# An expert's scatter in eight pieces between the next expert's gate and up products, and the next gather ahead of the SwiGLU transposes

## The chip, the cores and the metric

One NeuronCore of a Trainium2 chip runs the whole layer in one launch. Its engines run their own instruction streams and meet at semaphores: TensorE (PE in the profile, PEld for its weight loads), VectorE (DVE), ScalarE (ACT), GpSimd (POOL), and SyncE (SP), which here only issues transfers (DMA). The metric is the device time of one execution in microseconds (us). A profile is taken of one execution; its span runs from that execution's first to its last instruction.

## The reference, cut to what matters

The layer has an attention half, which the change does not touch, and an expert half, which is computed for 512 tokens of 1024 elements in float32:

```python
def expert_choice_ffn(h, w_router, w_gate, w_up, w_down):
    B, S, D = h.shape
    cap = EC_CAPACITY_FACTOR * S // N_EXPERTS          # 64
    aff = jax.nn.softmax((h @ w_router).astype(jnp.float32), axis=-1)
    gate, idx = lax.top_k(jnp.swapaxes(aff, 1, 2), cap)
    bidx = jnp.arange(B)[:, None, None]
    xe = h[bidx, idx]
    hid = (jax.nn.silu(jnp.einsum('becd,edf->becf', xe, w_gate))
           * jnp.einsum('becd,edf->becf', xe, w_up))
    ye = jnp.einsum('becf,efd->becd', hid, w_down) * gate[..., None].astype(h.dtype)
    return jnp.zeros_like(h).at[bidx, idx].add(ye)

# in the layer:
h2 = rmsnorm(x, g_norm_ffn[l]) * (1.0 + sc2) + sh2
x = x + gt2 * expert_choice_ffn(h2, w_router[l], w_gate[l], w_up[l], w_down[l])
return rmsnorm(x, g_final)
```

There are 16 experts. Each takes its 64 best tokens, multiplies them by a gate and an up matrix of 1024 x 2048 and a down matrix of 2048 x 1024, and adds the 64 rows back into the tokens' rows.

## The kernel before

The expert half starts once the router's positions are known. Tokens lie on 128 partitions in NT = 4 tiles: `x1` is the residual, `xn` its normalised copy, `pos` the place that a token has in an expert (or none). The loop over `e` in range(16) does for each expert:

- *Selection* (L1095 to L1097, DVE): `gw`, a 0/1 matrix of tokens by 64 places, one instruction for each token tile. The tile has one buffer.
- *Gather* (L1098 to L1102, PE): `px` = selected rows of `xn`, 8 matmuls.
- *Rows* (L1103 to L1111): DVE copies px to `xe`, PE transposes it (four transposes into a `tpb` bank of PSUM), DVE scales and shifts it into `xT`, the stationary operand of gate and up. `xT` has two buffers.
- *Scatter matrix and gate values* (L1113 to L1123): PE transposes `gw`, ACT casts it to `se`; PE multiplies `gw` by the affinities, DVE copies the result to `gv`.
- *Gate and up products* (L1125 to L1135, PE): for c in 0..3 a pass over a slot of gate weights into `pg`, then a pass over a slot of up weights into `pu`, 8 matmuls each. The profile counts a float32 matmul as two.
- *SwiGLU* (L1136 to L1144): Silu on ACT, product on DVE, eight transposes on PE, copies on ACT to `hT`.
- *Down product* (L1147 to L1152, PE): four passes over four slots of down weights into `py`.
- *ye* (L1154 to L1160): DVE scales `py` by `gv` and the layer's gate into `yf`; ACT and DVE split it in two parts that a faster float32r matmul takes, `ye`.
- *Scatter* (L1161 to L1166): eight times a matmul `se` x `ye` into one of two `tpb` banks (PE), and an addition into `x1` (DVE).

Each expert's weights come in 12 transfers of 2 MB (8 for gate and up in turns, 4 for down), into a ring of nine slots of 128 x 4096 floats (`we`; L984 and L996). SP issues them in ring order, and waits with each until PE has used what lay in its slot. The ring is filled for the first time (L999) before the router is done. The last expert's down weights come in 12 smaller transfers (L990), and its down product goes by column groups (L1172 to L1205), whose scatter, final norm and output follow. The last expert has no scatter of the kind above.

The text of the loop isn't the order on the engines: the framework puts each engine's instructions in an order of its own, by a timeline that it estimates, and inserts waits where tiles are reused. So the next expert's gather already stands between the gate and up passes of the one before it.

Of the kernel before, what the change touches and what calls it, by code (L numbers as in the profile page):

```python
# [9 lines left out]
F32 = mybir.dt.float32  # L10
# [4 lines left out]
OP = mybir.AluOpType  # L15
# [86 lines left out]
def tile_block(ctx, tc, x, c, positions, w_ada, b_ada, g_norm_mix, w_in, g_q_lat, g_kv_lat, w_uq, w_ukv,  # L102
# [968 lines left out]
    with ExitStack() as pb_:  # L1071
# [4 lines left out]
        for dh in range(2):  # L1076
            SP.dma_start(gt2[64 * dh:64 * dh + 64],
                         mod_d[5 * D + 512 * dh:5 * D + 512 * dh + 512].unsqueeze(0).to_broadcast([64, 512]))
        for e in range(E_N):
# [12 lines left out]
            wd = [w_.rearrange("p (r d) -> p r d", r=4) for w_ in wl[8:]]  # L1092

            gw = wbs.tile([P, NT, 2, CAP], F32, name="gw", bufs=1)
            for j in range(NT):  # L1095
                V.tensor_scalar(gw[:, j], iota[:, None, :].to_broadcast([P, 2, CAP]), pos[:, j, e:e + 1], None,  # L1096
                                op0=OP.is_equal)  # L1097
            px = ps.tile([P, 512], F32, name="px", bufs=1)  # L1098
            for j in range(NT):
                for dh in range(2):  # L1100
                    T.matmul(px[64 * dh:64 * dh + 64], gw[:, j, 0], xn[:, j, 512 * dh:512 * dh + 512],  # L1101
                             start=j == 0, stop=j == NT - 1)  # L1102
            xe = wbs.tile([P, 4, P], F32, name="xe", bufs=1)  # L1103
            V.tensor_copy(xe, px.rearrange("q (p r) -> q r p", r=4))  # L1104
            pt = ps.tile([P, 512], F32, name="tpb", bufs=2)
            for n in range(4):
                T.transpose(pt[:, 128 * n:128 * n + 128], xe[:, n], ident)
            xT = wbs.tile([P, KD, CAP], F32, name="xT", bufs=2)
            V.tensor_tensor(xT.rearrange("p (h n) s -> p n h s", h=2), pt.rearrange("p (n h s) -> p n h s", n=4, h=2),
                            a2c.rearrange("p (h n) -> p n h", h=2)[:, :, :, None].to_broadcast([P, 4, 2, CAP]), op=OP.mult)  # L1110
            V.tensor_tensor(xT, xT, sh2c[:, :, None].to_broadcast([P, KD, CAP]), op=OP.add)  # L1111
# [12 lines left out]

            pg = ps.tile([P, 2, 512], F32, name="pg", bufs=1)  # L1125
            pu = ps.tile([P, 2, 512], F32, name="pu", bufs=1)
            for c in range(4):
                for w_, acc in ((wg[c], pg), (wu[c], pu)):
                    for r in range(2):
                        k = 2 * c + r  # L1130
                        for b in range(2):
                            for hf in range(2):
                                f0 = 1024 * b + 512 * hf
                                T.matmul(acc[64 * hf:64 * hf + 64, b], xT[:, k], w_[:, r, f0:f0 + 512],  # L1134
                                         start=k == 0, stop=k == KD - 1)  # L1135
            hid = wbs.tile([P, 2, 4, P], F32, name="hid", bufs=1)  # L1136
            hT = wbs.tile([P, 4, 4, CAP], F32, name="hT", bufs=1)
            for b in range(2):
                A.activation(hid[:, b], pg[:, b].rearrange("q (p r) -> q r p", r=4), AF.Silu)  # L1139
                V.tensor_mul(hid[:, b], hid[:, b], pu[:, b].rearrange("q (p r) -> q r p", r=4))  # L1140
                pt = ps.tile([P, 512], F32, name="tpb", bufs=2)
# [6 lines left out]
            for g in range(4):  # L1148
                for r in range(4):
                    for dh in range(2):  # L1150
                        T.matmul(py[64 * dh:64 * dh + 64], hT[:, g, r], wd[g][:, r, 512 * dh:512 * dh + 512],  # L1151
                                 start=g == 0 and r == 0, stop=g == 3 and r == 3)  # L1152

# [7 lines left out]
            for dh in range(2):  # L1161
                for j in range(NT):
                    pt = ps.tile([P, 512], F32, name="tpb", bufs=2)
# [76 lines left out]
```

## Time and profile before

| what | value |
|---|---|
| median of 3 runs (lowest, highest) | 1939.73 us (1934.15, 1940.28) |
| the profiled execution | 1937.67 us |
| its span | 1935.9 us |
| mean granted TensorE clock | 0.926 |
| busy PE, DVE, ACT, POOL | 1777.8, 739.9, 395.4, 156.0 us |
| bytes moved | 531.20 MB, mean 274 GB/s |
| expert half in the span | from 938.1 us (first gather) to the end |

The page cuts the span into 40 slices and gives the busy share of each engine in tenths, the granted clock and the bytes moved; the expert half is the last 20 slices and part of the one before. A row of a timeline gives the start, the length, engine, line, operation, `output<-input` tiles and their shapes, the number of instructions merged in it, and in brackets the idle time before it and what ended it. A row of stretches gives the start and end, the length, busy time and count for PE, PEld, DVE, ACT and POOL, then the granted clock (1.00 is full speed), the share of the 16 DMA engines' time and GB/s. A row of waits reads "engine line waited for: us in total, times, longest".

### The profile page before, as it was taken

To read this page: it belongs to the slowest core of one execution; us is meant where nothing else is said; L and a number is where in the kernel's file an instruction comes from. 1 tells how busy PE (TensorE), PEld (TensorE's weight loads), DVE (VectorE), ACT (ScalarE), POOL (GpSimd) and SP (SyncE) were. 2 spreads that over 40 slices of the span, in tenths; PEclk is the share of its full clock that TensorE was granted. 3 is DMA by queue.
4 is the path that set the end of the run, shared out by engine and by line. 5 is a ranking of instruction groups with operands and counts; after the bars stand their busy time and mean duration, and the time that the engine had idled before them with its cause. 6 is when DMAs were issued, how large, how long until landed. Compare 5 with 4: busy or idle time off the path is not lost.

```text
span 1935.9 us, 21457 instructions
## 1 busy us (share of the span) xinstructions
PE 1777.8 (92%) x8812; PEld 1058.4 (55%) x8812; DVE 739.9 (38%) x1384; ACT 395.4 (20%) x769; POOL 156.0 (8%) x140
## 2 busy tenths in 40 slices
PE   4699999999999999999699999999999999999995
PEld 1466667888888888888233333334333343333332
DVE  6567865556454354445322022211222012220213
ACT  2345643322232322333000000000000000000002
POOL 6710000020020020010200000000000000000002
PEclk7799999999999999999799988899888988889888
DMA  8346666535533234234799999999999999999983
GB/s 268 92 134 212 220 200 199 154 121 154 179 102 119 66 88 122 88 109 177 312 428 427 419 407 406 399 429 403 404 403 424 407 406 406 405 429 405 406 355 93
DMA packets 133537, 531.20 MB, mean 274 GB/s; under 512 B 16952, under 2 KB 93880, under 8 KB 105792
## 3 DMA queue, kind: packets, MB, share of 16 engines
q1 hardware_dynamic: 131360, 523.02, 70.4%
q0 software_dynamic: 2080, 6.82, 0.9%
q8 instruction: 69, 1.13, 0.2%
q14 instruction: 28, 0.23, 0.0%
HBM read 520.45 MB, written 16.17 MB: 277 GB/s over the span
## 4 chain that ended last, share of the span: by engine, by line
PE 84%; DVE 8%; DMA 3%; ACT 2%; issue 2%; SPq 1%; ACTq 0%; DVEq 0%
PE pj L459 20%; PE pg L1134 13%; PE pu L1134 11%; PE py L1151 11%; PE pj L813 5%; PE pj L554 3%; PE px L1101 3%; PE tpb L1164 2%; PE sc L554 2%; DVE x L1166 2%; PE sc L884 1%; PE tpb L1120 1%; DMA raw<-in_w_ada_dram 1%; PE sc L659 1%; DMA y<-in_x_dram 1%
## 5 line engine op out<-in xcount | busy, mean ns | idle before, releaser
L459 PE MATMUL pj<-hh,ws 128*128 128x512 f32 x1248 | 406.4, 401 | 13.7 <-ACT ws L415 8.4
L459 PEld LDWEIGHTS pj<-hh,ws 128*128 128x128 f32 x1248 | 235.7, 189 | 74.4 <-ACT ws L415 8.6
L1134 PE MATMUL pg<-we,xT 128*64 128x512 f32 x1024 | 267.4, 655 | 0.0
L459 PE MATMUL pj<-hl,ws 128*128 128x512 f32 x624 | 249.7, 400 | 3.2 <-DVE hl L449 3.2
L1134 PE MATMUL pu<-we,xT 128*64 128x512 f32 x1024 | 237.3, 592 | 0.0
L1151 PE MATMUL py<-we,hT 128*64 128x512 f32 x960 | 209.3, 594 | 2.6 <-ACT hT L1144 1.1
L416 DVE TENSOR_TENSOR ws<-raw,ws 128x1024 fp32r<-128x1024 f32 (+2 forms) x114 | 141.0, 1239 | 146.7 <-ACT ws L415 146.2
L415 ACT ACTIVATE ws<-raw 128x1024 fp32r<-128x1024 f32 (+2 forms) x114 | 117.0, 1030 | 272.2 <-PE pj L459 188.6
L1134 PEld LDWEIGHTS pg<-we,xT 128*64 128x64 f32 x1024 | 86.2, 151 | 151.8 <-issue 151.5
L1134 PEld LDWEIGHTS pu<-we,xT 128*64 128x64 f32 x1024 | 83.1, 137 | 137.9 <-issue 137.6
L1151 PEld LDWEIGHTS py<-we,hT 128*64 128x64 f32 x960 | 67.6, 137 | 134.6 <-issue 128.5
L459 PEld LDWEIGHTS pj<-hl,ws 128*128 128x128 f32 x624 | 118.1, 189 | 30.5 <-DVE hl L449 3.9
L1164 PE MATMUL tpb<-ye,se 128*128 128x512 f32 x120 | 76.8, 726 | 49.5 <-DVE ye L1160 35.8
L1140 DVE TENSOR_TENSOR hid<-hid,pu 128x512 f32<-128x512 f32 x32 | 20.6, 684 | 243.5 <-PE pu L1134 243.5
L1139 ACT ACTIVATE hid<-pg 128x512 f32<-128x512 f32 x32 | 17.4, 594 | 470.1 <-PE pg L1134 470.1
L1104 DVE COPY xe<-px 128x512 f32<-128x512 f32 x16 | 11.1, 692 | 259.0 <-PE px L1101 259.0
L1155 DVE SCALAR_TENSOR_TENSOR yf<-py,gv,gt 128x512 f32<-128x512 f32 x15 | 11.3, 751 | 221.6 <-PE py L1151 221.6
L813 PE MATMUL pj<-ws,hh 128*128 128x256 f32 x512 | 94.4, 282 | 0.0
L1164 PEld LDWEIGHTS tpb<-ye,se 128*128 128x128 f32 x120 | 31.5, 275 | 100.4 <-issue 59.1
L1166 DVE TENSOR_TENSOR x<-x,tpb 128x512 f32<-128x512 f32 x120 | 78.0, 685 | 14.9 <-PE tpb L1164 13.5
L813 PEld LDWEIGHTS pj<-ws,hh 128*128 128x128 f32 x512 | 79.3, 188 | 0.0
L1101 PE MATMUL px<-xn,gw 128*64 128x512 f32 x256 | 75.8, 613 | 2.0 <-DVE gw L1096 2.0
(331 smaller groups left out, 1941.1 us busy)
## 6 DMA issues: line engine op xcount, KB each, us to landing
we<-in_w_gate_dram SPq DMA_DIRECT2D x64, 2048.0 KB, 15.6
we<-in_w_up_dram SPq DMA_DIRECT2D x64, 2048.0 KB
we<-in_w_down_dram SPq DMA_DIRECT2D x60, 2048.0 KB, 9.3
raw<-in_w_in_dram SPq DMA_DIRECT2D x38, 1024.0 KB, 5.3
raw<-in_w_ada_dram SPq DMA_DIRECT2D x22, 1024.0 KB, 6.9
x<-bkt_d SPq DMA_DIRECT2D x104, 128.0 KB, 4.1
raw<-in_w_in_dram SPq DMA_DIRECT2D x16, 512.0 KB, 5.3
stage_d<-stage POOLq DMA_DIRECT2D x26, 256.0 KB, 4.9
```

Of the source, the lines that this page charges most:

```text
L415: A.activation(dst[:, 0], src, AF.Copy)
L416: V.tensor_sub(dst[:, 1], src, dst[:, 0].bitcast(F32))
L459: T.matmul(pu, parts[k // 4][:, a, k % 4, col:col + 128], hx[b][:, k], start=k == 0 and n == 0, stop=k == KD - 1 and n == 2)
L554: T.matmul(out_, w_(a), b_(b), start=i == 0, stop=i == n_ - 1)
L659: T.matmul(pp[hh_], q_[hh_][:, a, qs], k_[hh_][:, b], start=n == 0, stop=False)
L813: T.matmul(pu[:, 256 * j:256 * j + 256], hx[b][:, k, 128 * m:128 * m + 128], parts[k // 4][:, a, k % 4], start=k == 0 and n == 0, stop=k = ...
L1101: T.matmul(px[64 * dh:64 * dh + 64], gw[:, j, 0], xn[:, j, 512 * dh:512 * dh + 512], start=j == 0, stop=j == NT - 1)
L1134: T.matmul(acc[64 * hf:64 * hf + 64, b], xT[:, k], w_[:, r, f0:f0 + 512], start=k == 0, stop=k == KD - 1)
L1140: V.tensor_mul(hid[:, b], hid[:, b], pu[:, b].rearrange("q (p r) -> q r p", r=4))
L1151: T.matmul(py[64 * dh:64 * dh + 64], hT[:, g, r], wd[g][:, r, 512 * dh:512 * dh + 512], start=g == 0 and r == 0, stop=g == 3 and r == 3)
L1164: T.matmul(pt, se[:, j], ye[:, dh], start=True, stop=True)
L1166: V.tensor_add(x1[:, j, ds_], x1[:, j, ds_], pt)
```

## The change

The selection, the gather, the rows and a piece of the scatter become functions of their own, and the loop calls them at other places: the first expert's selection, gather and rows ahead of its products; each later expert's selection and gather in the expert before it, after the SwiGLU products and ahead of their transposes, and its rows behind the first pass of the down product. The scatter of an expert moves into the next one: after each of the eight passes of gate and up stands one of its eight pieces. The scatter matrix and gate values of an expert now come after its gate and up passes. Nothing in what is computed changes; the additions into `x1` come in another order of column halves and tiles, on different elements.

```diff
+        def scatter(se, ye, j, dh):
+            pt = ps.tile([P, 512], F32, name="tpb", bufs=2)
+            T.matmul(pt, se[:, j], ye[:, dh], start=True, stop=True)
+            ds_ = slice(512 * dh, 512 * dh + 512)
+            V.tensor_add(x1[:, j, ds_], x1[:, j, ds_], pt)
+
         for e in range(E_N):
...
-            gw = wbs.tile([P, NT, 2, CAP], F32, name="gw", bufs=1)
...
-            V.tensor_tensor(xT, xT, sh2c[:, :, None].to_broadcast([P, KD, CAP]), op=OP.add)
+            if e == 0:
+                gw = select(0)
+                xT = rows(gather(0, gw))
+
+            pg = ps.tile([P, 2, 512], F32, name="pg", bufs=1)
+            pu = ps.tile([P, 2, 512], F32, name="pu", bufs=1)
+            for c in range(4):
+                for i, (w_, acc) in enumerate(((wg[c], pg), (wu[c], pu))):
+                    for r in range(2):
...
+                                T.matmul(acc[64 * hf:64 * hf + 64, b], xT[:, k], w_[:, r, f0:f0 + 512],
+                                         start=k == 0, stop=k == KD - 1)
+                    if e:
+                        scatter(se, ye, c, i)
...
             for b in range(2):
                 A.activation(hid[:, b], pg[:, b].rearrange("q (p r) -> q r p", r=4), AF.Silu)
                 V.tensor_mul(hid[:, b], hid[:, b], pu[:, b].rearrange("q (p r) -> q r p", r=4))
+            if e < E_N - 1:
+                gw = select(e + 1)
+                px = gather(e + 1, gw)
+            for b in range(2):
                 pt = ps.tile([P, 512], F32, name="tpb", bufs=2)
                 for n in range(4):
                     T.transpose(pt[:, 128 * n:128 * n + 128], hid[:, b, n], ident)
...
+                if g == 0:
+                    xT = rows(px)
...
-            for dh in range(2):
-                for j in range(NT):
-                    pt = ps.tile([P, 512], F32, name="tpb", bufs=2)
-                    T.matmul(pt, se[:, j], ye[:, dh], start=True, stop=True)
-                    ds_ = slice(512 * dh, 512 * dh + 512)
-                    V.tensor_add(x1[:, j, ds_], x1[:, j, ds_], pt)
```

`select`, `gather` and `rows` hold the lines of before word for word (L1094 to L1111). In the changed kernel the lines are: selection L1084, gather L1092, xe L1099, its transposes L1102, xT L1104 and L1106, scatter L1111 and L1113, gate and up L1142, transposes of gw L1149, gate values L1154 and L1157, SwiGLU L1161, L1162 and L1169, down L1177, yf and ye L1183 to L1188.

What the framework makes of it is seen in the engines' orders. First TensorE, where one expert ends and the next (here the fourth) begins. Before:

```order
L1151 MATMUL py<-we_7950,hT 64x512 x8
L1164 MATMUL tpb<-ye,se 128x512 x8
L1107 MATMUL tpb<-cs,xe 128x128 x4
L1115 MATMUL tpb<-cs,gw 128x128 x4
L1120 MATMUL tpb<-aff,gw 128x1 x4
L1134 MATMUL pg<-we_8138,xT 64x512 x8
L1134 MATMUL pu<-we_8140,xT 64x512 x8
```

The same place in the changed kernel (`we_` with a number is a slot's content):

```order
L1177 MATMUL py<-we_7950,hT 64x512 x8
L1142 MATMUL pg<-we_8138,xT 64x512 x8
L1111 MATMUL tpb<-ye,se 128x512 x4
L1142 MATMUL pu<-we_8140,xT 64x512 x8
L1111 MATMUL tpb<-ye,se 128x512 x4
L1142 MATMUL pg<-we_8142,xT 64x512 x8
L1149 MATMUL tpb<-cs,gw 128x128 x4
L1154 MATMUL tpb<-aff,gw 128x1 x4
L1092 MATMUL px<-xn,gw 64x512 x4
L1142 MATMUL pu<-we_8144,xT 64x512 x8
L1092 MATMUL px<-xn,gw 64x512 x4
L1142 MATMUL pg<-we_8146,xT 64x512 x8
```

The down product is followed at once by the next gate pass. The eight pieces of the scatter come in two groups of four behind the first two passes, not one behind each; the transposes of gw and the gate values stand behind the third pass, and the gather beside the fourth. In every other expert the groups are 2, 4 and 2, and the gather is one group of eight behind the fourth pass. The second expert alone has its pieces spread over passes three to eight.

Then TensorE around the down product, before:

```order
L1134 MATMUL pg<-we_8150,xT 64x512 x8
L1101 MATMUL px<-xn,gw 64x512 x3
L1134 MATMUL pu<-we_8152,xT 64x512 x8
L1101 MATMUL px<-xn,gw 64x512 x5
L1143 MATMUL tpb<-cs,hid 128x128 x8
L1151 MATMUL py<-we_8154,hT 64x512 x8
L1151 MATMUL py<-we_8156,hT 64x512 x8
```

and in the changed kernel:

```order
L1142 MATMUL pg<-we_8150,xT 64x512 x8
L1142 MATMUL pu<-we_8152,xT 64x512 x8
L1169 MATMUL tpb<-cs,hid 128x128 x8
L1177 MATMUL py<-we_8154,hT 64x512 x8
L1102 MATMUL tpb<-cs,xe 128x128 x4
L1177 MATMUL py<-we_8156,hT 64x512 x8
```

The gather has left the last passes, and the transposes of xe, which stood behind the scatter, now stand behind the first down pass. Last, VectorE over one expert, before:

```order
L1155 SCALAR_TENSOR_TENSOR yf<-py,gv,gt_7523 128x512
L1160 TENSOR_TENSOR ye<-yf,ye 64x512 x2
L1166 TENSOR_TENSOR x_67<-x_67,tpb 128x512 x8
L1109 TENSOR_TENSOR xT<-tpb,a2c 128x4x2x64
L1111 TENSOR_TENSOR xT<-xT,sh2c 128x512
L1123 COPY gv<-tpb 128x1
L1096 TENSOR_SCALAR gw<-cs,pos 128x128 x4
L1104 COPY xe<-px 128x512
```

and in the changed kernel:

```order
L1183 SCALAR_TENSOR_TENSOR yf<-py,gv,gt_7523 128x512
L1188 TENSOR_TENSOR ye<-yf,ye 64x512 x2
L1113 TENSOR_TENSOR x_67<-x_67,tpb 128x512 x8
L1157 COPY gv<-tpb 128x1
L1084 TENSOR_SCALAR gw<-cs,pos 128x128 x4
L1099 COPY xe<-px 128x512
L1162 TENSOR_TENSOR hid<-hid,pu 128x512 x2
L1104 TENSOR_TENSOR xT<-tpb,a2c 128x4x2x64
L1106 TENSOR_TENSOR xT<-xT,sh2c 128x512
```

The two steps that make xT have moved from between scatter and gate values to behind the SwiGLU product (`hid`). SP's order of transfers, and POOL's instructions, are the same in both kernels.

More of the change, by code (lines that the diff above doesn't have):

```diff
@@ L1078, in tile_block, with select, gather, rows @@
                          mod_d[5 * D + 512 * dh:5 * D + 512 * dh + 512].unsqueeze(0).to_broadcast([64, 512]))
+        def select(e):
+            gw = wbs.tile([P, NT, 2, CAP], F32, name="gw", bufs=1)
+            for j in range(NT):
+                V.tensor_scalar(gw[:, j], iota[:, None, :].to_broadcast([P, 2, CAP]), pos[:, j, e:e + 1], None,
+                                op0=OP.is_equal)
+            return gw
+        def gather(e, gw):
+            px = ps.tile([P, 512], F32, name="px", bufs=1)
+            for j in range(NT):
+                for dh in range(2):
+                    T.matmul(px[64 * dh:64 * dh + 64], gw[:, j, 0], xn[:, j, 512 * dh:512 * dh + 512],
+                             start=j == 0, stop=j == NT - 1)
+            return px
+        def rows(px):
+            xe = wbs.tile([P, 4, P], F32, name="xe", bufs=1)
+            V.tensor_copy(xe, px.rearrange("q (p r) -> q r p", r=4))
+            pt = ps.tile([P, 512], F32, name="tpb", bufs=2)
+            for n in range(4):
+                T.transpose(pt[:, 128 * n:128 * n + 128], xe[:, n], ident)
+            xT = wbs.tile([P, KD, CAP], F32, name="xT", bufs=2)
+            V.tensor_tensor(xT.rearrange("p (h n) s -> p n h s", h=2), pt.rearrange("p (n h s) -> p n h s", n=4, h=2),
+                            a2c.rearrange("p (h n) -> p n h", h=2)[:, :, :, None].to_broadcast([P, 4, 2, CAP]), op=OP.mult)
+            V.tensor_tensor(xT, xT, sh2c[:, :, None].to_broadcast([P, KD, CAP]), op=OP.add)
+            return xT
+        def scatter(se, ye, j, dh):
+            pt = ps.tile([P, 512], F32, name="tpb", bufs=2)
+            T.matmul(pt, se[:, j], ye[:, dh], start=True, stop=True)
+            ds_ = slice(512 * dh, 512 * dh + 512)
+            V.tensor_add(x1[:, j, ds_], x1[:, j, ds_], pt)
         for e in range(E_N):
@@ L1092, in tile_block @@
             wd = [w_.rearrange("p (r d) -> p r d", r=4) for w_ in wl[8:]]
[L1094 to L1111 removed]
+            if e == 0:
[6 more added lines that the diff above has]
+                    for r in range(2):
+                        k = 2 * c + r
+                        for b in range(2):
+                            for hf in range(2):
+                                f0 = 1024 * b + 512 * hf
+                                T.matmul(acc[64 * hf:64 * hf + 64, b], xT[:, k], w_[:, r, f0:f0 + 512],
+                                         start=k == 0, stop=k == KD - 1)
+                    if e:
+                        scatter(se, ye, c, i)
             pt = ps.tile([P, 512], F32, name="tpb", bufs=2)
@@ L1140, in tile_block @@
                 V.tensor_mul(hid[:, b], hid[:, b], pu[:, b].rearrange("q (p r) -> q r p", r=4))
+            if e < E_N - 1:
+                gw = select(e + 1)
+                px = gather(e + 1, gw)
+            for b in range(2):
                 pt = ps.tile([P, 512], F32, name="tpb", bufs=2)
```

14 lines of the change are left out of this document (removed).

## The prediction

> **What bounds the kernel now.** The page's slices come first, for the stage; the sequence of 16 experts fills the second half of the span. The reader should see that in it the DMA row is at 9 and the rate about 400 to 430 GB/s, while PE is at 9 as well.
>
> ```profile
> PE   4699999999999999999699999999999999999995
> DMA  8346666535533234234799999999999999999983
> GB/s 268 92 134 212 220 200 199 154 121 154 179 102 119 66 88 122 88 109 177 312 428 427 419 407 406 399 429 403 404 403 424 407 406 406 405 429 405 406 355 93
> ```
>
> Two resources look full, so the second view is the chain of waits over one expert, for its period and its pieces (start, length, what).
>
> ```profile
> 1678.46 1.80 PE tpb L1120 x8
> ...
> 1739.90 1.80 PE tpb L1120 x8
> 1741.69 5.25 PE pg L1134 x16
> 1746.94 3.43 PE pu L1134 x16
> ...
> 1771.03 3.45 PE pu L1134 x16
> 1774.57 0.70 DVE hid L1140
> 1776.69 13.98 PE py L1151 x64
> 1790.70 0.76 DVE yf L1155
> ...
> 1793.03 0.78 PE tpb L1164
> ...
> 1799.36 1.11 PE tpb L1107 x4
> 1800.48 0.85 PE tpb L1115 x4
> ```
>
> The period is 1739.90 − 1678.46 = 61.44 us, and PE's own chain carries all of it. After the end of py (1776.69 + 13.98 = 1790.67) the next pg pass starts at 1741.69 + 61.44 = 1803.13: for 12.5 us PE does no weight matmul. They are 2.36 us until ye is there, 6.33 us of scatter (1793.03 to 1799.36) and 3.8 us of transposes and gv. Then the first pg pass takes 5.25 where each later one takes 3.43.
>
> The third view, stretches of 2 us (near the end of a row: granted clock, DMA share, GB/s), tells both halves of the story.
>
> ```profile
> 1742.00:1744.00 2.00, 2.00 (x6) 0.47 (x4) 0.67 (x4) 0.00 (x0) 0.00 (x0) 0.50 1.00 426
> ...
> 1746.00:1748.00 2.00, 2.00 (x12) 0.62 (x10) 0.00 (x0) 0.00 (x0) 0.00 (x0) 1.00 0.38 107
> ...
> 1792.00:1794.00 2.00, 0.97 (x2) 0.50 (x2) 1.53 (x3) 0.80 (x2) 0.00 (x0) 0.70 0.98 418
> 1794.00:1796.00 2.00, 1.62 (x3) 0.58 (x2) 1.71 (x3) 0.00 (x0) 0.00 (x0) 0.50 1.00 426
> ```
>
> The clock falls to 0.50 in the scatter and is still there in the first pg pass. And the DMA engines run dry once per expert, here from 1746 on. Why they do is in SP's queue and in the table of waits:
>
> ```profile
> 1746.98 7.20 SPq L996 DMA_DIRECT2D we<-in_w_down_dram  x3
> SPq L996 <- PE pg L1134: 320.9, 30, 32.2
> PEld pu L1134 <- DMA we<-in_w_down_dram: 0.3, 1, 0.3
> ```
>
> SP waits for PE to free a slot of the ring of nine (320.9 us at this line alone); PE almost never waits for a transfer (0.3 us). PE frees nothing between the end of py and the end of the first pg pass, 12.5 + 5.25 us, and the queue empties. So the bound is PE's sequence, with the transfers 4% behind it. That "4%" needs their undisturbed rate: stretches without a dry spot, first and last of the twelve that lie between 1077 and 1806:
>
> ```profile
> 1077.00:1130.00 53.00, 49.52 (x206) 18.60 (x204) 11.83 (x21) 4.00 (x7) 0.00 (x0) 0.88 1.01 428
> ...
> 1751.00:1806.00 55.00, 50.59 (x214) 21.69 (x212) 11.57 (x21) 4.06 (x7) 0.00 (x0) 0.88 1.01 429
> ```
>
> A slot is 128 x 4096 x 4 bytes = 2.097 MB; at 428.5 GB/s 4.894 us, twelve of them 58.73 us per expert. The new kernel cannot go below that.
>
> **PE's period after the change.** The order listing shows the scatter as two groups of four, behind the first pg and the first pu pass (or 2, 4, 2). The prices at full clock are from the first expert, where these steps took less than in the chain above, and from the fastest scatter matmul (the first of its three durations):
>
> ```profile
> 944.89 0.66 PE L1107 MATMUL tpb<-cs,xe 128*128 128x128 f32 x4 [0.78 <-DVE xe L1104]
> 945.38 0.60 PE L1115 MATMUL tpb<-cs,gw 128*128 128x128 f32 x4
> 946.40 1.05 PE L1120 MATMUL tpb<-aff,gw 128*128 128x1 f32 x8 [0.42 <-DVE xT L1109]
> 947.57 0.87 DVE L1096 TENSOR_SCALAR gw<-cs,pos 128x128 f32<-128x128 f32 x4
> L1164 PE MATMUL tpb<-ye,se x120: 390/776/796, 996.1 to 1859.8; 128*128 128x512 f32 x120
> 975.07 3.43 PE px L1101 x16
> 1793.03 1.19 PE L1164 MATMUL tpb<-ye,se 128*128 128x512 f32 x2 [2.39 <-DVE ye L1160]
> 1793.84 1.28 DVE L1166 TENSOR_TENSOR x<-x,tpb 128x512 f32<-128x512 f32 x2 [0.23 <-PE tpb L1164]
> ```
>
> - Unchanged: 8 x 3.43 = 27.4 of gate and up, 13.98 of down, 3.43 of px, 2.2 from the last pu to py (1774.48 to 1776.69).
> - The 2.36 us until ye go to nothing: they run beside the first pg pass (3.43). Were that cover gone they would cost 15 x 2.36 = 35 us.
> - Scatter: with two tpb buffers the third piece waits for the first add. A group of four is then 0.39 + 2 x 0.64 (two adds) + 0.39, some 2.2 us with a little latency; at the pace of before, two pieces per 1.6 us, it is 3.0. Two groups are 4.4 to 6.0; I take 5.0, nearer the warm row, since weight matmuls surround them.
> - Transposes and gv: 0.66 + 0.60 + 1.05 = 2.3.
> - A new wait: gw has one buffer, so the next gather waits for gv to have read it and for the first selections (0.87 for four). In half of the experts px stands right behind gv, with pu, pg and all later PE work queued behind it: 0.2 to 1.1 us, I take 0.5. DVE's xe copy waits for px ahead of the SwiGLU product, which isn't due until the last pu.
> - The first pg pass at full clock: 5.25 becomes 3.43, −1.82.
>
> The sum is 27.4 + 13.98 + 3.43 + 2.2 + 5.0 + 2.3 + 0.5 = 54.8 us, with the ends 53.9 to 56.4. That is below 58.73, so what is late next is the transfer: PE overtakes its lead in the course of the experts and then waits for weights, some 1.5 us at a slot (4.894 − 3.43). SP's own order of issues, POOL's work and every transfer's size stay as they were; nothing is moved past either queue.
>
> **The time, then, is the transfers' path.** Its ends are read from these rows (SP's queue, stretches, PE):
>
> ```profile
> 951.08 7.19 SPq L996 DMA_DIRECT2D we<-in_w_down_dram  x3
> 950.00:955.00 5.00, 5.00 (x26) 1.72 (x24) 0.00 (x0) 0.00 (x0) 0.00 (x0) 1.00 0.59 200
> 1871.00:1874.00 3.00, 3.00 (x18) 0.98 (x16) 0.00 (x0) 0.00 (x0) 0.00 (x0) 1.00 0.89 313
> 1892.00:1895.00 3.00, 2.14 (x13) 0.68 (x10) 1.03 (x2) 0.00 (x0) 0.00 (x0) 1.00 0.86 272
> 1910.12 1.95 PE L1182 MATMUL py<-we,hT 128*64 128x256 f32 x16
> ```
>
> The first nine slots are filled before the stage. The tenth is issued at 951.08, when the first pg pass ends; the first expert is ordered as before up to there, so this stays. Data flow from 952.05 (0.59 of the five microseconds). 179 whole slots follow (192 less nine less the last four): 179 x 4.894 = 876.0, to 1828.1. The final gain's 0.52 MB adds 1.2. The last four slots, in twelve smaller transfers, took 1871.3 to 1894.6, 23.3 us: to 1852.6; about 1 us to be seen, as at the start. The last slot is first used at 1910.12, and from there to the span's end it is 1935.9 − 1910.1 = 25.8. Span 1879.4. The profiled execution took 1937.67, that is 1.8 more than its span, and 2.1 less than the median of the runs shown; so **1881 us**, 58 below that median. Per expert 2.7 us of dry queue go, some 40 in all; the other 16 or so come from the end: when the last transfer landed, PE still had all four slots of down weights before it, and now will have one.
>
> PE must also be in time: the second expert's pg starts at 994.4 instead of 1005.26, from
>
> ```profile
> 979.76 13.98 PE py L1151 x64
> ...
> 1005.26 3.58 PE pg L1134 x16
> 1896.10 7.09 PE L1182 MATMUL py<-we,hT 128*64 128x512 f32 x32
> ```
>
> and 979.76 + 13.98 + 0.66; fourteen periods p, the last expert's 36.3 up to its py (27.4 + 5.0 + 1.65 + 2.2) and 39.8 (1896.10 to the end) make 1070.5 + 14 p. PE sets the end only if p is over 57.8.
>
> **The clock, where it could go wrong.** The trace shows that PE idle for 2.39 us, followed by a scatter with gaps, costs the full clock, and that 2.2 us with transposes in it (1774.48 to 1776.69) do not. A starved PE idles 1.5 us in 4.9, less than either. In the Trainium skill, "TensorE: Matmul & The Clock Gate", section "HAM oscillation — how this bites in real kernels", bursts of matmuls that a transfer wait of over 3.4 us parts start each at half clock, which speaks against a kernel that waits for its weights. By it waits of 1.5 us cost nothing and the sum stays; were it to bite at 1.5 us too, twelve cold passes would make p 54.8 + 12 x 1.82 = 76.6. The trace is already stricter than the page, as its clock fell after 2.39 us.
>
> **Rivals.**
> 1. *Interrupted passes run cold.* Each such pass costs 1.82 us (5.25 against 3.43). With two or three per expert p is 58.4 to 60.3 and the span 1888 to 1915. For it: the first pg pass of today. Against: every gap is now framed by passes of 3.43 us at full rate. 13%, 1890 to 1917 us.
> 2. *The same, slower than before.* If both scatter groups, the gather's wait, the step to py and the ye hand-over each make a pass cold, p is 54.8 + 5 x 1.82 = 63.9 and the time 1967. It decides at p = 61.8, nearly four cold passes. But a PE that is late isn't starved, which takes starvation off the list. 5%.
> 3. *The change frees nothing.* The dry spot is not PE's doing, or the scheduler's order gives it back: 1938. SP's waits for PE and the listing speak against it. 5%.
> 4. *Deeper queues run slower.* Transfers now land 15.6 us after their issue, three slots' time, as the page has it:
>
> ```profile
> we<-in_w_gate_dram SPq DMA_DIRECT2D x64, 2048.0 KB, 15.6
> ```
>
> Up to nine will stand in line. A loss of 1 or 2% is 9 to 18 us: 1890 to 1899. 4%.
> 5. *They run faster.* A queue that never empties may gain as it may lose; 1.5% are 13 us, and with an end 3 us shorter (the groups ahead of the last slot are done by then) the time is 1865. No stretch of 50 us shows it. 4%. In the Trainium skill, "DMA: Bandwidth & Descriptors", section "Specifications", the fabric's ceiling is 435 GB/s, 1.5% above the measured 428.5, and by it 179 slots would take 13 us less.
>
> **The numbers.** My forecast has 69%, and its own range is 1872 to 1890. The likeliest time is 1881. To hold 8 in 10 the range takes in a third to a half of rival 1 and most of rival 4: 1866 to 1908. Under 0.3% (6 us) this kernel's measurement cannot tell a difference: faster 0.90, same 0.05, slower 0.05.
>
> **What would show it.** Right: DMA share 1.0 without dry spots from 952 on, its end near 1853; a period of 54 to 56 us early and 58.7 late; PE waiting for DMA of we in the later experts; clock 1.0 in nearly all stretches; SP's 320.9 us gone. Wrong: periods of 58 to 61 with the clock at 0.5 behind the scatter groups; a share of 1.0 with fewer GB/s; px waiting on gw for over 1.1 us.

## The result, and the profile after

The changed kernel takes 1887.74 us, the median of 4 runs (1883.85 to 1889.47); the kernel before took 1940.01 us beside it (4 runs, 1934.15 to 1940.9). The ratio is 0.9734, with a 95% interval of 0.9709 to 0.9759. Run again beside two of the later experiments it took 1884.85 against 1936.75 us, ratio 0.9732 (0.9715 to 0.9748). The profiled execution took 1883.85 us, with a span of 1882.1 us and a mean granted clock of 0.978 (0.926 before).

First the page's slices of the changed kernel, as they were read of before:

```profile
PE   4699999999999999999699999999988998889985
PEclk7799999999999999999799999999999999999998
DMA  9346766535534233231879999999999999999996
GB/s 273 89 130 197 244 194 191 179 107 162 166 112 126 90 90 104 90 90 68 363 331 427 426 428 428 428 426 427 428 428 427 427 428 428 428 427 427 427 424 203
```

In the second half the rate no longer swings between 399 and 429 GB/s; it stands at 424 to 428 in every full slice. PE has fallen from 9 to 8 in six slices late in the span: it is PE that waits now. The table of waits says for whom (SP's queue, then PE; us in total, times, longest):

```profile
SPq L984 <- DMA we<-in_w_down_dram: 159.8, 39, 5.8
...
SPq L996 <- PE pg L1142: 74.7, 15, 32.0
...
PE py L1177 <- DMA we<-in_w_down_dram: 18.4, 17, 2.2
PE pg L1142 <- DMA we<-in_w_gate_dram: 14.7, 12, 1.3
...
PE pu L1142 <- DMA we<-in_w_up_dram: 6.0, 8, 1.3
```

SP's 320.9 us of waiting for PE's gate passes at the down slots (L996) have become 74.7. PE waits 39.1 us for weights, in 37 waits, where it waited next to nothing. More than half of SP's other waiting is now put down to an earlier transfer: one lands 37.2 us after its issue (15.6 before), which is 37.2 / 4.89 = 7.6 transfers in line.

The chain of waits gives the periods. From the changed kernel, the starts of the first pg pass of five experts, between two of them one scatter group and the new wait for gw, and a pass that stands out:

```profile
1050.24 3.43 PE pg L1142 x16
...
1104.37 3.43 PE pg L1142 x16
1107.80 0.45 PE tpb L1111
...
1110.12 3.58 PE pu L1142 x16
...
1120.19 0.80 PE tpb L1154 x8
...
1121.17 0.20 DVE gw L1084
...
1121.42 1.94 PE px L1092 x8
...
1159.18 3.43 PE pg L1142 x16
...
1286.43 5.30 PE pu L1142 x16
...
1564.43 3.65 PE pg L1142 x16
...
1682.19 3.65 PE pg L1142 x16
```

The early periods are 54.1 and 54.8 us (1050.24, 1104.37, 1159.18); the late ones, where PE waits for weights, are (1682.19 − 1564.43) / 2 = 58.9 us, the twelve transfers of an expert. The first pg pass takes 3.43, not 5.25. One pass of the whole stage is cold, the pu pass at 1286.43; it is the only place between 955 and 1825 us where the granted clock of ten us is under 0.95. A scatter group takes 1110.12 − 1107.80 = 2.3 us. The ye that it needs was finished beside the pg pass, as the timeline has it (1105.92 + 1.40 = 1107.32):

```profile
1105.92 1.40 DVE L1188 TENSOR_TENSOR ye<-yf,ye 64x512 fp32r<-64x512 f32 x2 [0.76 <-ACT ye L1187]
```

Last, the two ends of the expert stage: SP's issue of the tenth slot, the last up slot in the chain, and PE's rows behind it.

```profile
950.32 7.19 SPq L996 DMA_DIRECT2D we<-in_w_down_dram  x3
...
1800.87 35.50 DMA we<-in_w_up_dram
...
1836.41 3.65 PE L1142 MATMUL pu<-we,xT 128*64 128x512 f32 x16 [1.26 <-DMA we<-in_w_up_dram]
1840.93 1.25 PE L1169 MATMUL tpb<-cs,hid 128*128 128x128 f32 x8 [0.86 <-DVE hid L1162]
1842.31 7.09 PE L1204 MATMUL py<-we,hT 128*64 128x512 f32 x32
1850.31 1.95 PE L1204 MATMUL py<-we,hT 128*64 128x256 f32 x16 [0.91 <-DVE yf L1206]
```

After the last up slot has landed (1800.87 + 35.50 = 1836.37), PE waits for no transfer any more: the brackets name only DVE. From there to the end of the span are 45.7 us.

From SP's issue of the tenth slot to the end are 1882.1 − 950.32 = 931.8 us; before it was 1935.9 − 951.08 = 984.8. This length is a better yardstick than the time for what follows. In the four profiles of the changed kernel and its near relatives (below) it is 931.7, 931.8, 931.8 and 931.9, while the tenth slot is issued anywhere from 948.87 to 952.44; over all profiles of this study with whole slots that point lies between 948.87 and 957.50 us. So the spread of a few us from one execution to the next seems to come from the part ahead of the experts, which is the same in all of them.

### The profile page after: what moved, and what is told of

The parts are those of the page before. It is cut to its first block, busy times and chain, and to the rows that moved or that the text cites. A ratio compares the mean times of both kernels' runs of the same rounds, so it can differ in the third digit from the quotient of the medians.

```text
span 1882.1 us, 21443 instructions
## 1 busy us (share of the span) xinstructions
PE 1716.5 (91%) x8812; PEld 996.9 (53%) x8812; DVE 738.9 (39%) x1384; ACT 395.3 (21%) x769; POOL 155.4 (8%) x140
## 4 chain that ended last, share of the span: by engine, by line
PE 64%; DMA 25%; DVE 6%; SPq 2%; issue 1%; ACT 1%; ACTq 0%; DVEq 0%; POOL 0%; POOLq 0%
PE pj L459 21%; DMA we<-in_w_up_dram 11%; DMA we<-in_w_gate_dram 10%; PE pu L1142 8%; PE pg L1142 8%; PE pj L813 5%; PE py L1177 4%; PE pj L554 3%; PE px L1092 2%; PE sc L554 2%; DVE x L1113 2%; PE sc L884 2%; PE tpb L1111 1%; DMA x<-bkt_d 1%; DMA raw<-in_w_ada_dram 1%
## 5 line engine op out<-in xcount | busy, mean ns | idle before, releaser
L1142 PE MATMUL pg<-we,xT 128*64 128x512 f32 x1024 | 233.4, 595 | 14.7 <-DMA we<-in_w_gate_dram 14.7
L1142 PE MATMUL pu<-we,xT 128*64 128x512 f32 x1024 | 236.7, 599 | 6.0 <-DMA we<-in_w_up_dram 6.0
L1177 PE MATMUL py<-we,hT 128*64 128x512 f32 x960 | 216.3, 597 | 20.3 <-DMA we<-in_w_down_dram 18.4
L1142 PEld LDWEIGHTS pg<-we,xT 128*64 128x64 f32 x1024 | 73.0, 137 | 156.2 <-issue 131.0
L1142 PEld LDWEIGHTS pu<-we,xT 128*64 128x64 f32 x1024 | 72.3, 137 | 147.8 <-issue 133.4
L1177 PEld LDWEIGHTS py<-we,hT 128*64 128x64 f32 x960 | 66.4, 137 | 150.3 <-issue 126.9
L1113 DVE TENSOR_TENSOR x<-x,tpb 128x512 f32<-128x512 f32 x120 | 77.4, 685 | 127.4 <-PE tpb L1111 127.4
L1162 DVE TENSOR_TENSOR hid<-hid,pu 128x512 f32<-128x512 f32 x32 | 20.6, 684 | 219.1 <-PE pu L1142 219.1
L1161 ACT ACTIVATE hid<-pg 128x512 f32<-128x512 f32 x32 | 17.4, 595 | 299.1 <-PE pg L1142 299.1
L1183 DVE SCALAR_TENSOR_TENSOR yf<-py,gv,gt 128x512 f32<-128x512 f32 x15 | 11.3, 751 | 155.2 <-PE py L1177 155.2
L1187 ACT ACTIVATE ye<-yf 64x512 fp32r<-64x512 f32 x30 | 18.8, 628 | 252.1 <-DVE yf L1183 251.7
L813 PE MATMUL pj<-ws,hl 128*128 128x256 f32 x256 | 71.6, 280 | 0.0
L1092 PE MATMUL px<-xn,gw 128*64 128x512 f32 x256 | 61.2, 614 | 4.6 <-DVE gw L1084 4.6
## 6 DMA issues: line engine op xcount, KB each, us to landing
we<-in_w_gate_dram SPq DMA_DIRECT2D x64, 2048.0 KB, 37.2
```

What stands on the lines that cost most here:

```text
L813: T.matmul(pu[:, 256 * j:256 * j + 256], hx[b][:, k, 128 * m:128 * m + 128], parts[k // 4][:, a, k % 4], start=k == 0 and n == 0, stop=k = ...
L1113: V.tensor_add(x1[:, j, ds_], x1[:, j, ds_], pt)
```

## Experiments: which edit frees the products

The order of the instructions on PE, read after the result was known, suggested that the place given to the scatter's pieces might not be what mattered. A `tpb` bank is handed out in the order of the text. Before, the next expert's rows (the transposes of `xe`, L1107) ask for a tpb bank *behind* the scatter's eight pieces, so they, and with them all of the next expert's products, must come after the scatter. The *turn theory* says that this turn alone made the block; the *placing theory* says that the block goes only if the scatter is written between the products. Four kernels tell them apart. (The kernel before took 1937.42 us beside these four.)

**rows_last**: the changed kernel with its early gather, but the scatter in one block and the rows called behind it.

```diff
-                    if e:
-                        scatter(se, ye, c, i)
...
-                if g == 0:
-                    xT = rows(px)
...
+            for dh in range(2):
+                for j in range(NT):
+                    scatter(se, ye, j, dh)
+            xT = rows(px)
```

> The changed kernel with its functions and its early gather, but with the scatter called in one block behind ye and the rows called behind the scatter. Theory (turn): the transposes of xe stand behind the scatter's pieces in the turns of tpb again, the engines' order is that of the kernel before, and the time is 1932 to 1945 us. Rival (placing; the early gather has a part of its own): 1890 to 1925 us.

Measured: 1939.92 us, ratio 1.0009 (0.9994 to 1.0024). The gain is gone, though selection and gather stand early. On PE stands, between the down product of one expert and the next expert's products:

```
L1175 MATMUL py<-we_7764,hT 64x512 x8
L1111 MATMUL tpb<-ye,se 128x512 x8
L1102 MATMUL tpb<-cs,xe 128x128 x4
...
L1142 MATMUL pg<-we_7952,xT 64x512 x8
```

SP waits for PE as it did before (table of waits):

```profile
SPq L996 <- PE pg L1142: 323.6, 30, 31.8
```

**gather_only**: the changed kernel with the scatter in one block behind ye, but the rows left where the change has them (the first and the third piece of the diff above, without the second and without the last line).

> Only the selection, gather and rows are moved ahead; the scatter stands in one block at the end of its own expert. Theory (turn): the rows have had their turn in tpb before the scatter starts, so the framework mixes the scatter with the next expert's passes by itself: 1882 to 1894 us. Rival (placing): the scatter in one block keeps the 12 us gap at the hand-over: 1925 to 1940 us.

Measured: 1886.08 us, ratio 0.9742 (0.9725 to 0.9759), 931.9 us from the tenth issue to the end. With the rows' turn ahead of the scatter, the framework spreads the pieces between the next expert's passes by itself; on PE stand now

```
L1175 MATMUL py<-we_7760,hT 64x512 x6
L1102 MATMUL tpb<-cs,xe 128x128 x4
L1175 MATMUL py<-we_7760,hT 64x512 x2
L1175 MATMUL py<-we_7762,hT 64x512 x8
L1175 MATMUL py<-we_7764,hT 64x512 x8
L1142 MATMUL pg<-we_7952,xT 64x512 x8
L1111 MATMUL tpb<-ye,se 128x512 x2
L1142 MATMUL pu<-we_7954,xT 64x512 x8
L1111 MATMUL tpb<-ye,se 128x512 x3
```

**scatter_only**: the changed kernel with selection, gather and rows back at the head of the loop; only the scatter's pieces stay between the next expert's passes, and with them, behind the expert's own passes, its scatter matrix and gate values.

> Only the scatter is moved into the next expert's products; selection, gather and rows stand at the head of each expert as before. Theory (turn): the rows are ahead of the scatter in the turns of tpb, which is all that counts: 1882 to 1894 us, as the changed kernel. Rival (two parts that add up): some of the gain is the gather's, 1895 to 1920 us.

Measured: 1883.68 us, ratio 0.9735 (0.972 to 0.9751), 931.7 us. Either half of the change is enough, and both together bring no more: what they share is that the rows get their bank ahead of the scatter. They share the place of the scatter matrix and gate values too, but so does rows_last, which gains nothing.

**rows_py**: the kernel before, with one line changed: the rows' transposes use py's bank, which is free once yf is made, instead of a tpb bank.

```diff
-            pt = ps.tile([P, 512], F32, name="tpb", bufs=2)
+            pt = ps.tile([P, 512], F32, name="py", bufs=1)
             for n in range(4):
                 T.transpose(pt[:, 128 * n:128 * n + 128], xe[:, n], ident)
```

> The kernel before with one word changed: the four transposes of xe take their PSUM bank from py and not from the two tpb banks. Theory (turn): what kept the scatter in one block was that those transposes stood behind the scatter's eight pieces in the turns of tpb, so that xT, and with it every product of the next expert, had to wait for the last addition; freed of that the framework itself sets the scatter between the next expert's passes. Then PE's period is 54 to 57 us, the transfers bound the expert half and the time is 1884 to 1896 us. Rival (placing): the gain comes from the scatter written between the products and the early gather, which this kernel does not have: 1936 to 1942 us.

Measured: 1899.86 us, ratio 0.9803 (0.9782 to 0.9823). The turn theory is right in its direction, but the time lies above the 1884 to 1896 us that it had been given: the gain is not quite three quarters of the whole. Why the rest is missing, this kernel's chain, PE's timeline and a stretch (granted clock third from the end) show:

```profile
1509.44 13.98 PE py L1151 x64
...
1568.11 13.98 PE py L1151 x64
...
1586.51 6.62 PE pg L1134 x16
```

```profile
1524.25 0.66 PE L1107 MATMUL py<-cs,xe 128*128 128x128 f32 x4 [0.85 <-DVE yf L1155]
1526.41 0.73 PE L1164 MATMUL tpb<-ye,se 128*128 128x512 f32 x2 [1.50 <-DVE ye L1160]
1527.85 5.24 PE L1134 MATMUL pg<-we,xT 128*64 128x512 f32 x16 [0.71 <-DVE xT L1111]
```

```profile
1528.00:1530.00 2.00, 2.00 (x6) 0.62 (x8) 0.99 (x2) 0.00 (x0) 0.00 (x0) 0.50 0.98 418
```

From the end of py (1509.44 + 13.98) to the next pg pass are now 4.4 us instead of 12.5. In them PE idles three times, 0.85, 1.50 and 0.71 us, and works for 1.4; the clock falls to 0.50, and the pass behind runs cold, 5.24 us here and 6.62 in the next expert. The period is 1568.11 − 1509.44 = 58.7 us, so PE is no faster than the transfers. This is the first rival of the prediction, in a kernel in which its condition holds, with one such pass in each expert.

The transfers lose nothing by it: from 955 to 1825 us the share of busy DMA engines is 1.00, and the last transfer lands as long after the tenth issue as in the changed kernel, 908 us. But PE never catches up with them. The last up pass starts without a wait for its slot,

```profile
1854.96 3.60 PE L1134 MATMUL pu<-we,xT 128*64 128x512 f32 x16
```

which is 1854.96 − 955.92 = 899.0 us after this kernel's tenth issue, against 886.1 in the changed kernel. So the 13 us that are missing (the stage takes 944.9 us instead of 931.8) all lie at the end.

## Experiments: how much of it is the clock

The block costs in two ways: 12.5 us in which no weights are used, and the half clock in it and behind it. Two kernels keep the block and only keep PE busy in it.

**before_warm**: the kernel before, with two fill matmuls while PE waits for ye, and each scatter matmul done a second time, into px's bank.

```diff
+            fill = ps.tile([P, 512], F32, name="px", bufs=1)
+            for _ in range(2):
+                T.matmul(fill, ident, yf, start=True, stop=True)
...
                     T.matmul(pt, se[:, j], ye[:, dh], start=True, stop=True)
+                    T.matmul(fill, se[:, j], ye[:, dh], start=True, stop=True)
```

> The kernel before with PE kept busy in the hand-over: two matmuls of yf with the identity and a second copy of each scatter matmul, written to the px bank and read by nobody. They also push the gather into the scatter's block. Theory: of the 7 us by which PE's period fell, about 3 are the clock (first pg pass 1.8, transposes and gv 1.5); with them PE's period is 57 to 60 us and the time 1886 to 1915 us. Rival (the clock has no part, only the order has): the added work keeps the period at 61 us or makes it longer, 1935 to 1970 us.

Measured: 1892.41 us beside 1940.61, ratio 0.9754 (0.9728 to 0.978). But since px's bank is taken, the next gather moved into the block too (3.61 us of px at 1518.26, between scatter and rows), which leaves PE less to do later. So the clock isn't alone in this run, and it decides nothing by itself.

**before_fill**: the same idea with the fills in pg's bank, which is free until the next pg pass; the gather stays where it was.

```diff
+            fill = ps.tile([P, 2, 512], F32, name="pg", bufs=1)
+            for b in range(2):
+                T.matmul(fill[:, b], ident, yf, start=True, stop=True)
...
                     V.tensor_add(x1[:, j, ds_], x1[:, j, ds_], pt)
+                    if (dh, j) != (1, NT - 1):
+                        T.matmul(fill[:, 0, :256], ident, x1[:, j, 512 * dh:512 * dh + 256], start=True, stop=True)
```

> The kernel before, with the scatter in one block and the gather where it was; PE only gets 2 fill matmuls of 128x512 while it waits for ye and one of 128x256 after each of the first seven additions, all into pg's bank, which the next pg pass overwrites. If the cold clock is the larger part of what the block costs: the clock stays at 1.0 from the end of py to the next pg pass, that pass takes 3.4 to 3.6 us instead of 5.25, the scatter's eight pieces take some 5 to 6 us instead of 6.33, the period is 57.5 to 59.5 instead of 61.44 and the time 1886 to 1910. If the gather's move into the block was what gained in the run with the fillers in px: the period stays over 60.5 and the time is 1925 to 1950.

Measured: 1903.11 us beside 1936.75, ratio 0.9827 (0.9808 to 0.9847). In its chain and in one of its stretches:

```profile
1515.38 13.98 PE py L1151 x64
...
1541.30 3.58 PE pg L1134 x16
...
1600.55 3.58 PE pg L1134 x16
```

```profile
1534.00:1536.00 2.00, 1.88 (x10) 1.24 (x8) 1.48 (x3) 0.00 (x0) 0.00 (x0) 1.00 1.00 426
```

The block is as long as before (1515.38 + 13.98 to 1541.30 is 11.9 us against 12.5), but the clock stays at 1.00 in it, and the pass behind it takes 3.58. The period is 59.25 us instead of 61.44, and the stage is 32.6 us shorter than before (its tenth slot was issued at 955.04: 1907.2 − 955.04 = 952.2, against 984.8). So keeping the clock up is enough for some 33 of the 53 us, with the block still there; the other 20 come only when the block itself goes, and PE runs ahead until the transfers bind. The nine fill matmuls per expert that bring these 33 us make nothing that is used.

Where the gains lie is seen from the moment at which the transfers end. These are the last stretches of 1 us in which they still move (share of busy engines before the last number), in the kernel before, rows_py, before_fill and the changed kernel:

```profile
1894.00:1895.00 1.00, 0.28 (x3) 0.29 (x4) 1.00 (x2) 0.00 (x0) 0.00 (x0) 1.00 0.38 118
1863.00:1864.00 1.00, 1.00 (x8) 0.42 (x6) 0.00 (x0) 0.00 (x0) 0.00 (x0) 1.00 0.19 61
1865.00:1866.00 1.00, 0.16 (x2) 0.00 (x0) 0.72 (x2) 0.00 (x0) 0.00 (x0) 1.00 0.80 253
1857.00:1858.00 1.00, 1.00 (x12) 0.57 (x8) 1.00 (x2) 0.94 (x3) 1.00 (x2) 1.00 0.36 119
```

| kernel | tenth issue to the end of the transfers | from there to the end |
|---|---|---|
| before | 944 us | 41 us |
| rows_py (short block, clock falls) | 908 us | 37 us |
| before_fill (long block, clock stays) | 911 us | 41 us |
| changed | 908 us | 24 us |

Either remedy alone gives the transfers back nearly all of their 36 us, so the parts of clock and block don't add up. The 17 us at the end came, of these four, only in the changed kernel, where PE is faster than the transfers and has worked off its lag when the last of them lands.

## Experiments: what bounds the changed kernel

**gather_x2** and **gather_x3**: the changed kernel with the gather of experts 1 to 15 done two and three times over into the same bank, 3.43 us of PE work more per expert each time.

```diff
-            for j in range(NT):
-                for dh in range(2):
+            for _ in range(2 if e else 1):
+                for j in range(NT):
+                    for dh in range(2):
```

> The changed kernel with the gather of experts 1 to 15 done twice (the second result replaces the first, which is the same): 3.43 us more of PE work in each of 15 experts, 51 us in all. Theory (the transfers bound it): PE's period goes from 54.4 to 57.8 us, which is the point where PE would begin to set the end; the time rises by 0 to 5 us against the changed kernel (1884 to 1893 us). Rival (PE's work bounds it): plus 45 to 55 us, about 1937 us.

> As before with the gather done three times: 6.9 us more of PE work in each expert, 103 us in all. Theory (the transfers bound it, slack of 3.4 us per expert): PE's period is 61.3 us, PE is the bound, and the span is 993.7 + 6.9 + 14 x 61.3 + 76.1 = 1935 us: about 1937 us, plus 50 against the changed kernel. Rival (PE's work bounds it already): plus 95 to 105 us, about 1990 us.

Measured, beside 1940.61 us: gather_x2 1887.35 us, ratio 0.972 (0.9703 to 0.9737), and gather_x3 1940.66 us, ratio 1.0008 (0.9993 to 1.0022). The first pg passes in their chains (gather_x2, then gather_x3):

```profile
1058.46 3.43 PE pg L1143 x16
...
1116.47 3.43 PE pg L1143 x16
...
1174.70 3.43 PE pg L1143 x16
```

```profile
1498.47 3.43 PE pg L1143 x16
...
1560.17 3.43 PE pg L1143 x16
```

At a period of 58.0 to 58.2 us nearly all of the additional work is free (the stage takes 935.7 us instead of 931.8, for 51 us of matmuls); at 61.7 us all of the gain is gone. So PE has some 4 us in hand per expert, what lies between its own 54.8 and the transfers' 58.7.

**eleven_loads**: the changed kernel with one transfer less per expert; its down product reads the third slot twice.

```diff
+                if n == 11 and e < E_N - 1:
+                    wl.append(wl[10])
+                    continue
```

> The changed kernel without the fourth down transfer of experts 0 to 14 (its passes read the third slot again, so a part of the down product is another one): 15 transfers of 2 MB less, PE's work the same. Theory (the transfers bound it, PE close behind): the transfers' path would end 74 us earlier, PE's path with its period of 54.4 us gives a span of 993.7 + 14 x 54.4 + 76.1 = 1831 us: 1828 to 1840 us. Rival a (PE is the bound): no change, 1884 to 1890 us. Rival b (nothing but the transfers counts): 1810 to 1818 us.

Measured: 1837.33 us beside 1940.61, ratio 0.9458 (0.9439 to 0.9477), 1832.0 − 950.58 = 881.4 us for the stage. Its chain has a period of 54.1 us late in the stage:

```profile
1539.92 3.43 PE pg L1145 x16
...
1594.04 3.43 PE pg L1145 x16
```

That is 50 us less for 15 transfers less, and the period is PE's own again. Both directions agree: the changed kernel is bound by its transfers, and PE follows 4 us per expert behind.

**ring19**: a try to beat it. The ring of nine slots is cut into nineteen halves, so that half a slot more is loaded ahead and the first half comes free sooner. To make room, `xe` shares the buffer of `yf`, `xT` has one buffer instead of two, and `hid` is made in two halves.

```diff
-        wb = [ctx.enter_context(pool(f"wb{n}")) for n in range(9)]
+        wb = [ctx.enter_context(pool(f"wb{n}")) for n in range(19)]
...
-            return wb[n].tile([P, 4096], F32, name=f"we{n}")
+            return wb[n].tile([P, 2048], F32, name=f"we{n}")
```

> The changed kernel with its ring of nine slots cut into nineteen halves (transfers of 1 MB): half a slot more (2.45 us of transfer) is loaded ahead, and the first half is free one half pass (1.7 us) earlier. If the transfers' path sets the whole time, the dry time ahead of the tenth slot shrinks by about 4 us, and so does the span: 1876 to 1880, the time 1878 to 1885 beside the changed kernel's 1884 to 1889, ratio to the kernel before some 0.971. If transfers of half the size cost rate (0.5% is 4.4 us), or PE still sets a part of the time: the same as the changed kernel, or up to 8 us above it.

**after_again**: the changed kernel beside it.

> The changed kernel again, as the comparison on this chip: 1883 to 1890, ratio to the kernel before 0.971 to 0.976; the transfers of the expert stage end near 1856 and start near 950.

Measured, beside 1936.75 us: ring19 1896.19 us, ratio 0.9792 (0.9768 to 0.9816); the changed kernel 1884.85 us, as above. The stretch from 955 to 1825 us of both, ring19 first:

```profile
955.00:1825.00 870.00, 802.85 (x3612) 273.03 (x3608) 174.56 (x311) 61.64 (x105) 2.43 (x4) 1.00 1.01 421
```

```profile
955.00:1825.00 870.00, 802.43 (x3640) 281.88 (x3636) 172.86 (x311) 60.73 (x105) 2.44 (x4) 1.00 1.01 428
```

The transfers did start earlier (87 GB/s from 945 to 950 us, where the changed kernel moves nothing), but transfers of 1 MB with 8 KB per partition cost 1.7% of the rate, 421 against 428 GB/s at the same share of busy time, some 14 us over the stage; size and line length changed together, so this run doesn't tell which of the two it is. The expectation had put that loss at 0.5%, and the time ended above both of its cases. Nor do the additional slots lengthen the line: a transfer of down weights lands 19.8 us after its issue, which is 19.8 / 2.49 = 8 of these transfers, and in the changed kernel the longest takes 39.4 us, 8 of 2 MB. There the ring of nine slots may be the reason, in ring19 it can't be; what holds back the ninth transfer in ring19 no run here shows. No version here that does all of the work is clearly faster than the changed kernel.

**last_whole**: a test of the one term of the prediction that was off, the end of the transfers. The last down weights come in whole slots, so the last down product takes other columns of them.

```diff
-            elif e == E_N - 1:
-                for m in range(2):
...
             else:
                 k = 512 * (n - 8)
```

> The changed kernel with the last expert's down weights in four whole transfers of 2 MB with 16 KB lines instead of twelve small ones; its down product then takes other columns of the weights. In the changed kernel the last up slot lands at 1836.4, and transfers end near 1856.5. If the twelve small transfers, which share the engines with the last whole slots, delay these: the last up slot lands 2 to 6 us earlier after the transfers' start, transfers end near 1850 to 1853 at 420 GB/s and more, and the span is 2 to 6 us shorter (1876 to 1880), the time 1878 to 1884. If the last up slot's landing is set by the ring and the sum of the whole slots alone: it lands within 1 us of 1836.4, the end is PE's work behind it, 45.7 us, and the span stays at 1881 to 1883, the time 1883 to 1888.

Measured: 1888.41 us beside 1937.77, ratio 0.9742 (0.9719 to 0.9765). The profiled execution got to the tenth slot late, at 957.50, so it is read from there. The queue's row, the last up pass, and the last stretches (share and GB/s at the end):

```profile
957.50 3.77 SPq L988 DMA_DIRECT2D we<-in_w_down_dram  x2
```

```profile
1843.63 3.65 PE L1134 MATMUL pu<-we,xT 128*64 128x512 f32 x16 [1.24 <-DMA we<-in_w_up_dram]
```

```profile
1852.00:1855.00 3.00, 2.67 (x14) 0.89 (x12) 0.00 (x0) 0.00 (x0) 0.00 (x0) 1.00 1.02 426
1855.00:1858.00 3.00, 2.17 (x11) 0.52 (x6) 0.74 (x1) 0.00 (x0) 0.00 (x0) 1.00 0.77 328
1858.00:1861.00 3.00, 2.21 (x16) 1.36 (x18) 0.70 (x2) 0.63 (x1) 0.00 (x0) 1.00 0.49 208
1861.00:1864.00 3.00, 3.00 (x22) 1.62 (x18) 0.84 (x2) 0.12 (x1) 0.01 (x1) 1.00 0.15 66
```

The last up slot is used 1843.63 − 957.50 = 886.1 us after the tenth issue, and in the changed kernel 1836.41 − 950.32 = 886.1: the small transfers don't delay it, and the first theory falls. But the second had the end wrong too: the stage is 934.4 us long, 2.6 more than with the small transfers. PE idles 1.62 us until ye is there, a time that it fills with the next column group where that comes in small pieces, and waits 0.33 us for a down slot. What the stretches show besides is how the transfers end: not at once, but over some 9 us, in which the share of busy engines falls from 1.02 to 0.15. In the changed kernel the same is seen at its last whole slot, whose packets of 16 KB can be told from those of the small transfers behind it (the DMA view of short windows counts packets under 8 KB). Small packets move from 1829 us on (of the 146 packets up to 1831, 108 are under 8 KB, and only 13 of these, of other kinds, under 512 B), and packets of 16 KB still start after 1835, 2 of the 165 up to 1836; at 1836.4 the slot has landed. So the next transfers are under way for 7 us while the last parts of the slot come in.

## Why the prediction was right, step by step

- **The bound.** Right. PE's block starved SP's queue; with the block gone the dry spots are gone, and of the wait of 320.9 us 74.7 are left, 32.0 of them a single wait.
- **PE's period.** Predicted 54.8 us, measured 54.1 to 54.8. Its terms held one by one: two scatter groups 4.6 us for 5.0, the wait on gw 0.43 us (from 1120.19 + 0.80 to 1121.42) for 0.5, the wait for ye under the first pg pass, and that pass at 3.43.
- **The transfers' period.** Predicted 58.73 us, measured 58.9 late in the stage.
- **The two parts of the gain.** Predicted were some 40 us of dry queue and 16 at the end; the transfers end 36 us earlier after the tenth issue, and what lies behind them is 17 us shorter.
- **The clock.** The forecast took waits of some 1.5 us for a slot as harmless, and they were: with 37 waits of up to 2.2 us, the clock of the whole stretch from 955 to 1825 is 1.00. The one cold pass, of 5.30 us, followed a scatter group and the transposes of gw, not a wait for weights; the same steps with the same 0.55 us of idle time were followed by a pass of 3.58 us at 1070.11. The first rival's mechanism is real, as rows_py shows, but its condition, several idle spots in a row with little between them, doesn't come up here. The two kernels also bound the Trainium skill's rule of over 3.4 us ("TensorE: Matmul & The Clock Gate", section "HAM oscillation — how this bites in real kernels"): single waits of up to 2.2 us are harmless, as it has it, but three of at most 1.50 us within 4.4 were not. The next section of that page, "A second HAM failure mode: psum-queue depth-cycling", has frequent micro-idles as a cause of its own, and rows_py with its three idle spots agrees.
- **The second rival's point of turning.** Predicted at a period of 61.8 us; gather_x3 runs at 61.7 and takes the time of before.
- **Deeper queues** run neither slower nor faster: 428 GB/s with 7.6 transfers in line, 428.5 before.
- **The sum.** The stage was to last 1879.4 − 951.08 = 928.3 us and lasted 931.8. The step that was off is "The last four slots, in twelve smaller transfers, took 1871.3 to 1894.6, 23.3 us: to 1852.6", with the 25.8 us that were added behind it. The count of bytes is right, but not the moment at which a slot has landed: by the count the last up slot is there 878 us after the tenth issue, and it was used after 886.1. The first packets of the small transfers do move at 879 us (1829 − 950.32), but alongside the last of the whole slots, as last_whole's paragraph shows, and from there to 908 us, or 1858 and not 1852.6, the last four slots took some 29 us, not 23.3. And the end hangs on that up slot, with 45.7 us of work behind it: 886.1 + 45.7 = 931.8. The last down pieces, on which the sum was built, come just in time to cost nothing; that both ways agree within 4 us is partly luck. Of the 6.7 us between 1881 and 1887.74 the other 3.9 lie between the profiled execution and the median. For the kernel before the prediction named 2.1 us between these two, but its 1881 is the span plus 1.8, the time of a profiled execution, to which they were not added.
- **What the prediction didn't see** is which words of the change do it. It costed the scatter at its new place; the experiments show that the place is the framework's choice, and that the edit counts because the rows take their tpb bank ahead of the scatter.

Open stays what exactly makes PE's clock fall: 4.4 us with 1.4 of work in them did it in rows_py, the 2.2 us of the SwiGLU step with its transposes never, and a scatter group and the transposes and narrow matmuls of gw, with 0.55 us of idle time between them, did it once and not at other times.

## What to carry to other kernels

When work of one round blocks the next round, look for the buffer or bank that both take in turn before moving any code: the turn follows the order of the text, and one line that gives the next round's first step a bank of its own, or its turn earlier, can free everything behind it. Where the freed step then meets the next limit, here the transfers 4 us further on, nothing more is to be had on that engine, as 51 us of doubled work for almost nothing showed. And a gap in front of a long run of matmuls can cost twice, as time and as clock, and the two parts need not add up: here filling the gap with matmuls that nobody uses gave 33 of the 53 us, and closing most of it while the clock still fell gave 40.

## What the runs showed of the hardware

- The granted clock reacted to what PE did in the gap, not to its length alone: 11.9 us filled with small matmuls kept 1.00 (before_fill), 4.4 us with three idle spots of at most 1.50 gave 0.50 (rows_py).
- Transfers of 2 MB with 16 KB per partition moved 428 GB/s, those of 1 MB with 8 KB 421; with the last expert's small transfers, of 1 or 2 KB lines, among them the rate was 305 to 403 GB/s in stretches of 3 us, at nearly the same share of busy engines (0.95 to 1.05).
  The Trainium skill ("DMA: Bandwidth & Descriptors", section "Bandwidth") gives 341 GB/s for a transfer of 1 MB issued from GpSimd; those of ring19, issued from SyncE and in line behind others, moved 421.
- With 7.6 transfers in line each lands 37 us after its issue without loss of rate, but what is in line overlaps: the last whole slot came 8 us later than a count in order gives, with packets of the next transfers moving for 7 us beside its own.
